# The opening of a two-layer diffusion backbone: modulation vectors on TensorE, six feed-forward tiles fed before the norm is known

## The chip, the cores and the metric

The kernel runs on one NeuronCore of one Trainium2 chip. Its time is the device time of one execution in microseconds (us). All operands are 32-bit floats. The engines are called as the profile calls them: PE (TensorE, matrix products) with PEld (its weight loads), DVE (VectorE), ACT (ScalarE), POOL (GpSimd), and SP, whose queue issues the DMA transfers.

## What is computed

Two layers work on 384 tokens (128 of a context, 256 of a latent grid) of width 1024. Each layer is a half-step feed-forward block, a token mixer, and another half-step feed-forward block. Ahead of each block stands an RMS norm whose result is scaled and shifted by vectors that come from a condition vector:

```python
def modulation(cvec, w, b):
    m = jax.nn.silu(cvec) @ w + b
    return m.reshape(cvec.shape[0], N_SUB, 3, D_MODEL)

def sub_in(x, g, m, sidx):
    shift, scale = m[:, sidx, 0], m[:, sidx, 1]
    return rmsnorm(x, g[sidx]) * (1 + scale[:, None, :]) + shift[:, None, :]

def swiglu(h, w_gu, w_down):
    gt, up = jnp.split(h @ w_gu, 2, axis=-1)
    return (jax.nn.silu(gt) * up) @ w_down
```

Context tokens and latent tokens have a condition vector each, so every scale and shift exists twice. The first block needs the shift and the scale of sub-layer 0 (1024 values each, twice) before its input is complete. This case is about that opening.

## The kernel before

**Layout.** The activations stand transposed: `X` has 128 partitions (a slice of the width) by 8 blocks `k` by 384 tokens. A tile of weights is 128 x 1024, 512 KB; its eight 128 x 128 pieces belong to the eight blocks `k`.

**Products in three parts.** Every factor is split into a rounded part `hi` and a remainder `lo`. `weights` loads a tile (DMA), rounds it on ACT (`hi`) and subtracts on DVE (`lo`). The input is split in the same way into `hh` and `hl`. A product of one tile with one block, called a pair below, is then three matrix products: hi·hh, hi·hl, lo·hh, each with 384 token columns.

**Order.** Engines run their instructions in order. A scheduler sets that order from a simulated timeline and from dependences that the code adds by hand: `chain("pe", ...)` strings matrix products in the order in which the code issues them, `chain("fill", ...)` does so for DVE. In the opening the order is written in the string `SPROG`, a list of tokens, each a step on a block.

**The opening (`start`).** Before the change:

- `A`: DVE computes the scale of block 0; then `stats` sums the squares of all blocks on PE (`L294`) and DVE takes the reciprocal root. `N` (`norm_end`) spreads that over the partitions by three products (`L267`), and ACT copies it to `R`. The squares themselves are taken before, on ACT, and added on DVE (`L282`).
- `S k`: the shift of block `k`, six of the eight on PE. Eight products with the condition vector as weights (two columns) and the loaded tile `mc` (`mod_w`) as data give a row of 2 x 128; ACT copies the row (`L1063`). `T k` turns that row into a column by a small product with the identity; ACT adds the bias (`L1071`).
- `H k` (`gen`): the scale of block `k` on DVE: two products with sums over 1024 elements (`mod_dot`, `L203`), one for each condition vector, then `L1085`. The `lo` parts of the first six gate/up tiles (`L164`, tile `gr`) are strung in here. Then `hgen` makes the normalised, scaled and shifted input of block `k` and splits it.
- `P k` (`step`): pairs of the tiles whose turn `GUP` gives, with block `k`; a tile that joins late catches up. The six tiles hold six PSUM banks to the end.

After the opening `ffn` evacuates the six banks (`evac`) and runs the remaining gate/up tiles, two at a time (`plain`, `L176` to `L178`), on the complete `hh` and `hl`.

Other blocks of the same kernel begin differently (`head`): their first tiles work on the input before the norm (`X` times scale only), with two more columns that hold the shift (`AUG`, 386 columns). The banks are multiplied by `R` when they are evacuated (`ev`), and the complete input is made by `hgen` afterwards for the tiles that follow.

Of the kernel before, what the change touches and what calls it, by code (L numbers as in the profile page):

```python
# [86 lines left out]
class Net:  # L87
# [98 lines left out]

    def mod_pe(self, l, n):
        nc = self.nc
        raw = self.wp.tile([P, 1024], F32, tag="raw", name="raw", bufs=3)
        nc.sync.dma_start(raw, self.a["mod_w"][l, n])  # L190
        ps = self.misc()
        for k in range(KD):
            nc.tensor.matmul(ps[:, :2], lhsT=raw[:, k * P:(k + 1) * P], rhs=self.sT[:, k, :], start=k == 0, stop=k == KD - 1)
        st, k = divmod(n, KD)
        nc.vector.tensor_copy(self.mod[l, st // 3, st % 3][:, k, :], ps[:, :2])
# [74 lines left out]

    def square(self, m):
# [8 lines left out]
        nc.scalar.activation(q, self.X[:, m, :], AF.Square)  # L280
        if not first:
            nc.vector.tensor_tensor(out=self.acc, in0=self.acc, in1=q, op=ALU.add)  # L282

# [3 lines left out]

    def stats(self):
        nc = self.nc
        ps = self.misc()  # L290
        st = ps[:, N:]
        for i in range(3):
            c = slice(i * P, (i + 1) * P)
            self.chain("pe", nc.tensor.matmul(st[:, i:i + 1], lhsT=self.acc[:, c], rhs=self.ones[:, 0:1], start=True, stop=True))  # L294
# [716 lines left out]
    def start(self, B=6):  # L1011
        nc, a = self.nc, self.a
        mm = lambda *args, **kw: self.chain("pe", nc.tensor.matmul(*args, **kw))  # L1013
# [4 lines left out]
        if PB:
            cr = self.fp.tile([P, 1024], F32, tag="junk", name="junk", bufs=1)[0:2, :]
            sel = T_([2, 2, P], F32, name="sel")  # L1020
            nc.sync.dma_start(cr, a["cv"])
            nc.sync.dma_start(sel, a["sel"])
        nc.sync.dma_start(self.small, a["small"])
# [4 lines left out]
        nc.scalar.activation(self.sT.rearrange("p k v -> p (k v)"), self.sm("cvec"), AF.Silu)  # L1028
        if PB:
            nc.scalar.activation(cr, cr, AF.Silu)  # L1030
            for v in range(2):
                for c in (slice(0, 512), slice(512, 1024)):
                    b = self.bank()
                    nc.tensor.matmul(b, lhsT=sel[:, v, :], rhs=cr[:, c], start=True, stop=True)
                    nc.scalar.activation(self.sb[:, v, c], b, AF.Copy)
        else:
            self.load_cond()
        for k in range(KD):
            self.square(k)
# [4 lines left out]
        tiles = []
        for k in range(KD):
            for o, dst in ((KD, sc), (0, sh)):
                dst[k] = T_([P, D], F32, tag="mc", name="mc", bufs=12)
                nc.sync.dma_start(dst[k], a["mod_w"][0, o + k])
            for _ in range(GUP.count(k)):
                tiles.append(self.gu_tile(0, 0, len(tiles), T_([P, D], F32, tag="gr", name="gr", bufs=B)))  # L1050
# [4 lines left out]
        def shift(k, src=None):
            if src is None:
                if k >= SHP:
                    return
# [4 lines left out]
            nc.scalar.activation(row[k], tr[0:2, :P], AF.Copy)  # L1063

        def turn(k):
            if k >= SHP:
                self.mod_dot(0, k, sh[k])
                nc.vector.tensor_scalar(out=S[:, k, :], in0=S[:, k, :], scalar1=self.sm("mod_b", k, 1), scalar2=None, op0=ALU.add)
                return
            mm(tn[:, 2 * k:2 * k + 2], lhsT=row[k], rhs=self.ident[0:2, 0:2], start=True, stop=True)  # L1070
            nc.scalar.activation(S[:, k, :], tn[:, 2 * k:2 * k + 2], AF.Identity, bias=self.sm("mod_b", k, 1))  # L1071

        def scale(k):
            if k in CP:
                return
            self.mod_dot(0, KD + k, sc[k])
            scale_end(k, G[:, k, :])

        def scale_pe(k):
            mm(tn[:, 64 + 2 * k:64 + 2 * k + 2], lhsT=row[k], rhs=self.ident[0:2, 0:2], start=True, stop=True)  # L1080
            scale_end(k, tn[:, 64 + 2 * k:64 + 2 * k + 2])

        def scale_end(k, src):
# [1 line left out]
            nc.vector.scalar_tensor_tensor(out=G[:, k, :], in0=src, scalar=one[:, k:k + 1], in1=g, op0=ALU.add, op1=ALU.mult)  # L1085
# [23 lines left out]
        def first():  # L1109
            self.last["fill"] = None  # L1110
            scale(0)
            self.stats()

        def second():
            self.norm_end()
            self.last["fill"] = self.dg

        tn = None
        for tok in SPROG.split():
            k = int(tok[1:] or 0)  # L1120
            if tok[0] in "TD" and tn is None:
                tn = self.misc()
            {"S": lambda: shift(k), "C": lambda: shift(k, sc[k]), "D": lambda: scale_pe(k), "T": lambda: turn(k), "H": lambda: gen(k), "P": lambda: step(k),
             "A": first, "N": second}[tok[0]]()
        return banks
# [128 lines left out]
```

## Time and profile before

| | us |
|---|---|
| three runs, median | 1421.05 |
| three runs, lowest and highest | 1419.83, 1423.15 |
| profiled execution, its own time | 1424.8 |
| span of the profiled execution | 1423.0 |

| engine | busy us | share of the span |
|---|---|---|
| PE | 1390.6 | 98% |
| PEld | 1349.1 | 95% |
| DVE | 1076.7 | 76% |
| ACT | 657.0 | 46% |

PE is busy nearly all the time; weight loads run beside the products. The profiled execution took 3.75 us more than the median of the three runs. Times inside the profile count from the start of its span. A line such as L203 is a line of the kernel before; in the changed kernel the same function stands some lines higher or lower.

### The profile page before, as it was taken

To read this page: it belongs to the slowest core of one execution; us is meant where nothing else is said; L and a number is where in the kernel's file an instruction comes from. 1 tells how busy PE (TensorE), PEld (TensorE's weight loads), DVE (VectorE), ACT (ScalarE), POOL (GpSimd) and SP (SyncE) were. 2 spreads that over 40 slices of the span, in tenths; PEclk is the share of its full clock that TensorE was granted. 3 is DMA by queue.
4 is the path that set the end of the run, shared out by engine and by line. 5 is a ranking of instruction groups with operands and counts; after the bars stand their busy time and mean duration, and the time that the engine had idled before them with its cause. 6 is when DMAs were issued, how large, how long until landed. Compare 5 with 4: busy or idle time off the path is not lost.

```text
span 1423.0 us, 20761 instructions
## 1 busy us (share of the span) xinstructions
PE 1390.6 (98%) x7877; PEld 1349.1 (95%) x7877; DVE 1076.7 (76%) x1945; ACT 657.0 (46%) x1079; POOL 10.8 (1%) x25
## 2 busy tenths in 40 slices
PE   7999999999998999999999999999998999999997
PEld 4999999998887999999999999999998999999886
DVE  7799989977987798879858887897688675334324
ACT  5443433339985643333345333333677564333322
POOL 0000000000110000000000000000000000000000
PEclk9999999999999999999999999999999999999999
DMA  9377777762135387767725766675330335333431
GB/s 372 131 258 246 230 225 249 237 204 89 60 119 178 105 256 231 216 200 246 241 74 189 246 210 210 211 243 186 104 114 31 103 121 162 125 127 120 133 104 45
DMA packets 71484, 247.24 MB, mean 174 GB/s; under 512 B 7877, under 2 KB 10583, under 8 KB 71385
## 3 DMA queue, kind: packets, MB, share of 16 engines
q1 hardware_dynamic: 71384, 245.92, 53.4%
q8 instruction: 62, 1.02, 0.3%
q14 instruction: 38, 0.30, 0.1%
HBM read 244.03 MB, written 1.85 MB: 173 GB/s over the span
## 4 chain that ended last, share of the span: by engine, by line
PE 91%; ACT 3%; DVE 3%; DMA 1%; issue 1%; SPq 0%; DVEq 0%; ACTq 0%
PE b L178 25%; PE b L176 25%; PE b L177 25%; PE b L737 5%; PE b L492 5%; PE b L1013 2%; PE m L737 1%; ACT rrt L495 1%; ACT ttt L495 1%; DMA sb<-in_cv 1%; DVE lo L164 0%; DVE lo L499 0%; ACT L495 0%; DMA raw<-in_lru_w_out 0%; DMA X<-in_x 0%
## 5 line engine op out<-in xcount | busy, mean ns | idle before, releaser
L163 ACT ACTIVATE hi<-raw 128x1024 fp32r<-128x1024 f32 (+1 forms) x282 | 293.3, 1042 | 599.7 <-issue 307.8
L178 PE MATMUL b<-hh,lo 128*128 128x384 f32 (+1 forms) x1372 | 461.9, 337 | 0.0
L176 PE MATMUL b<-hh,hi 128*128 128x384 f32 (+1 forms) x1372 | 461.0, 338 | 0.0
L177 PE MATMUL b<-hh,hi 128*128 128x384 f32 (+1 forms) x1372 | 456.6, 333 | 0.0
L164 DVE TENSOR_TENSOR lo<-raw,hi 128x1024 fp32r<-128x1024 f32 (+1 forms) x282 | 338.0, 1200 | 147.9 <-ACT hi L163 144.7
L203 DVE CUSTOM_DVE_ANT_0 junk<-mraw,sb 128x1024 f32<-128x1024 f32 x256 | 312.5, 1221 | 6.3 <-DMA mraw<-in_mod_w 3.5
L177 PEld LDWEIGHTS b<-hh,hi 128*128 128x128 f32 x1372 | 258.2, 188 | 0.0
L178 PEld LDWEIGHTS b<-hh,lo 128*128 128x128 f32 x1372 | 257.5, 188 | 0.0
L176 PEld LDWEIGHTS b<-hh,hi 128*128 128x128 f32 x1372 | 257.4, 188 | 0.0
L176 PE MATMUL b<-hid,hi 128*128 128x384 f32 x528 | 176.4, 334 | 0.0
L177 PE MATMUL b<-hid,hi 128*128 128x384 f32 x528 | 176.4, 334 | 0.0
L178 PE MATMUL b<-hid,lo 128*128 128x384 f32 x528 | 176.4, 334 | 0.0
L176 PEld LDWEIGHTS b<-hid,hi 128*128 128x128 f32 x528 | 99.1, 188 | 0.0
L177 PEld LDWEIGHTS b<-hid,hi 128*128 128x128 f32 x528 | 99.1, 188 | 0.0
L178 PEld LDWEIGHTS b<-hid,lo 128*128 128x128 f32 x528 | 99.1, 188 | 0.0
L393 DVE TENSOR_TENSOR t<-t,b 128x384 f32<-128x384 f32 x79 | 43.5, 552 | 71.1 <-PE b L178 71.0
L492 PE MATMUL b<-hh,hi 128*128 128x386 f32 x328 | 89.4, 354 | 6.0 <-DVE X L499 5.8
L492 PEld LDWEIGHTS b<-hh,hi 128*128 128x128 f32 x328 | 61.5, 195 | 9.1 <-issue 5.6
L492 PE MATMUL b<-hh,lo 128*128 128x386 f32 x164 | 56.8, 346 | 0.0
L178 PE MATMUL b<-hi,hid 128*128 128x512 f32 x132 | 51.4, 389 | 0.0
L177 PE MATMUL b<-lo,hid 128*128 128x512 f32 x132 | 51.4, 389 | 0.0
L176 PE MATMUL b<-hi,hid 128*128 128x512 f32 x132 | 51.3, 389 | 0.0
(218 smaller groups left out, 1534.9 us busy)
## 6 DMA issues: line engine op xcount, KB each, us to landing
raw<-in_gu SPq DMA_DIRECT2D x170, 512.0 KB, 4.1
mraw<-in_mod_w SPq DMA_DIRECT2D x128, 512.0 KB, 4.3
raw<-in_down SPq DMA_DIRECT2D x48, 512.0 KB, 4.3
raw<-in_down_last SPq DMA_DIRECT2D x22, 512.0 KB, 3.6
raw<-in_down SPq DMA_DIRECT2D x24, 384.0 KB, 4.2
mc<-in_mod_w SPq DMA_DIRECT2D x16, 512.0 KB, 10.2
raw<-in_lru_w_in SPq DMA_DIRECT2D x16, 512.0 KB, 3.7
raw<-in_w_qkv SPq DMA_DIRECT2D x10, 512.0 KB, 3.9
```

What stands on the lines that cost most here:

```text
L163: nc.scalar.activation(hi[:, :cols], raw[:, :cols], AF.Copy)
L164: self.wlo = nc.vector.tensor_tensor(out=lo[:, :cols], in0=raw[:, :cols], in1=hi[:, :cols].bitcast(F32), op=ALU.subtract)
L176: first = mm(out, lhsT=lh, rhs=rh, start=start, stop=False)
L177: mm(out, lhsT=lh, rhs=rl, start=False, stop=False)
L178: self.end = mm(out, lhsT=ll, rhs=rh, start=False, stop=stop)
L203: i = nc.vector.tensor_tensor_reduce(out=junk, in0=raw, in1=self.sb[:, v, :], scale=1.0, scalar=0.0, op0=ALU.mult, op1=ALU.add, accum_out= ...
L393: nc.vector.tensor_tensor(out=x, in0=x, in1=bu[:, ALL], op=ALU.mult)
L492: return self.chain("pe", nc.tensor.matmul(*args, **kw))
L495: return self.chain("act", nc.scalar.activation(*args, **kw))
L737: return self.chain("pe", T.matmul(*args, **kw)) if PIN else T.matmul(*args, **kw)
L1013: mm = lambda *args, **kw: self.chain("pe", nc.tensor.matmul(*args, **kw))
```

## The change

The opening is rewritten, and nothing else:

- **Scale on PE.** All eight scale vectors (`c0` to `c7`) and three of the shift vectors (blocks 4, 6, 7, `SPE`) come from PE. The condition vector is widened to 32 columns (`sT`, 30 of them zero), and the eight products of a vector write to four strips of 32 PSUM partitions in turn, two to a strip (`rows`); such eight products are called a row set below. ACT copies the 128 x 128 result, and `turn`, one product with a 0/1 matrix `sel4`, adds the four strips and gives a column. It stands directly behind its row set on PE.
- **Shift on DVE.** The other five shift vectors (blocks 0, 1, 2, 3, 5) are computed on DVE by `mod_dot`, where the eight scale vectors and the shifts of blocks 6 and 7 were.
- **Input before the norm.** The six tiles no longer take the normalised input. `gen` makes `X` times scale; `bias` casts the shift to two more columns; `pair` uses 386 columns. The squares (`Q`), `stats` (`X`) and `norm_end` (`N`) move to the end of the opening. `L` does the last two blocks of all six tiles.
- **After the opening** `ffn` runs `hgen` for blocks 0 to 5, `ev` for the six banks (which multiplies by `R`), then `hgen` for blocks 6 and 7.
- **Loads** are issued in the order of `LOADS`: the small vectors first, then `X` in four parts between the weights.

The order of PE where the last blocks stand. Before, a row set (`mc`, `sT`) and a turned row (`ident`, `row`) stand between pairs, and the turned row is that of an earlier row set:

```order
L1013 MATMUL b_166<-mc_189,sT_81 2x128 x8
L1013 MATMUL m_289<-ident_78,row_287 128x2
L1013 MATMUL b_160<-hh_77,hi_173 128x384 x2
L1013 MATMUL b_160<-hh_77,lo_174 128x384
L1013 MATMUL b_166<-mc_199,sT_81 2x128 x8
L1013 MATMUL m_289<-ident_78,row_306 128x2
```

Now, ahead of the pairs of block 5, the sums of the squares and the row sets of shift 6 and scale 7, each with its own turn behind it:

```order
L283 MATMUL m_146<-ones_79,acc_258 128x1 x3
L1006 MATMUL b_145<-mc_215,sT_113 32x128 x8
L1006 MATMUL m_146<-sel4_112,row_518 128x2
L1006 MATMUL b_145<-mc_213,sT_113 32x128 x8
L1006 MATMUL m_146<-sel4_112,row_530 128x2
L1006 MATMUL b_139<-hh_77,hi_152 128x386 x2
L1006 MATMUL b_139<-hh_77,lo_153 128x386
```

What moved: the turn no longer follows other pairs, and the norm's sums, which stood ahead of everything, stand in the last third.

The end of the opening on PE, now: the spreading of the norm, the last row set, the first pair of `L`, and in it the first products of the first `plain` tile (`b_722`, weights `hi_718` and `lo_719`), which read the complete input of block 0:

```order
L254 MATMUL m_146<-dg_555,ones_79 128x128
L254 MATMUL m_146<-dg_558,ones_79 128x128
L1006 MATMUL b_145<-mc_217,sT_113 32x128 x8
L1006 MATMUL m_146<-sel4_112,row_577 128x2
L1006 MATMUL b_139<-hh_77,hi_152 128x386 x2
L1006 MATMUL b_139<-hh_77,lo_153 128x386
L173 MATMUL b_722<-hh_77,hi_718 128x384
L1006 MATMUL b_139<-hh_77,hi_152 128x386
L174 MATMUL b_722<-hh_77,hi_718 128x384
L175 MATMUL b_722<-hh_77,lo_719 128x384
```

What moved: before, the first `plain` product stood behind 108 products of the six tiles, on an input that had been complete since `H 0`; now 33 products of the six tiles stand behind it.

DVE at its beginning. Before: the sums of squares, then the dots of scale 0 (two `ISA` rows are one dot):

```order
L282 TENSOR_TENSOR acc<-acc,t 128x384 x6
L203 ISA junk,m_83<-mc,sb 128x1024
L203 ISA m_83 128x1
L282 TENSOR_TENSOR acc<-acc,t 128x384
```

Now: the scale from PE's result (`L1060`), the remainder of X times scale (`L1071`), the dots of a shift (`L190`), its cast, then the weights' remainder:

```order
L1060 SCALAR_TENSOR_TENSOR m_83<-m,one,small 128x2
L1071 SCALAR_TENSOR_TENSOR hh<-X,m_83,hh 128x128
L1071 SCALAR_TENSOR_TENSOR hh<-X,m_83,hh 128x256
L190 ISA junk,m_82<-mc,sb 128x1024
L190 ISA m_82 128x1
L190 ISA junk,m_82<-mc,sb 128x1024
L190 ISA m_82 128x1
L1077 TENSOR_SCALAR m_82<-m_82,small 128x2
L166 CAST hh<-m_82 128x2
L169 TENSOR_TENSOR hh<-m_82,hh 128x2
L161 TENSOR_TENSOR lo<-gr,hi 128x1024 x2
```

What moved: DVE's first work now waits for PE, and every block's dots stand between the scale of that block and the scale of the next.

DVE where the norm arrives: the last scaled remainders (`L1071`), then `X` times `R` for six blocks (`L317`, `L309`), the cast (`L166`) and the remainder (`L169`) of the complete input of block 0:

```order
L1071 SCALAR_TENSOR_TENSOR hh<-X,m_83,hh 128x256
L317 TENSOR_TENSOR t<-X,R 128x384 x2
L309 SCALAR_TENSOR_TENSOR t<-X,m_83,R 128x128
L309 SCALAR_TENSOR_TENSOR t<-X,m_83,R 128x256
L317 TENSOR_TENSOR t<-X,R 128x384 x3
L166 CAST hh<-t 128x384
L166 CAST hh<-m_82 128x2
L166 CAST hh<-t 128x384
L314 SCALAR_TENSOR_TENSOR hh<-t,m_82,hh 128x128
L314 SCALAR_TENSOR_TENSOR hh<-t,m_82,hh 128x256
L169 TENSOR_TENSOR hh<-t,hh 128x384
```

What moved: these stood in the blocks `H 0` to `H 5`; now they follow each other at the end, behind `N`.

On ACT the order of the first steps changed too: before, the table load has no wait and is followed by the condition vector's activation; now the table load stands behind the wait for the transfer of `small`.

The diff, cut to what matters here:

```diff
-XO = [slice(0, 4), slice(4, 8)]
-SHP = 6
-GUP = (0, 1, 2, 3, 4, 5)
-SPROG = "A S0 N S1 T0 H0 S2 T1 H1 P0 S3 T2 H2 P1 S4 T3 H3 P2 S5 T4 H4 P3 T5 H5 P4 P5 T6 H6 T7 H7 P6 P7"
+SPE = (4, 6, 7)
+GUP = (0, 0, 1, 2, 3, 3)
+LOADS = "x0 c0 g0 c1 s0 g1 x2 c2 s1 g2 x4 c3 s2 g3 x6 c4 s3 g4 c5 s4 g5 c6 s5 c7 s6 s7"
+SPROG = "C0 T0 H0 C1 T1 H1 B0 Q0 Q1 C2 T2 P0 H2 B1 Q2 Q3 C3 T3 P1 H3 B2 C4 T4 P2 H4 B3 Q4 Q5 S4 U4 C5 T5 P3 H5 B4 Q6 Q7 C6 T6 P4 X H6 B5 S6 U6 C7 T7 P5 N B6 H7 S7 U7 B7 L"
...
         elif banks:
-            for j in range(hp):
-                evac(j, *banks[2 * j:2 * j + 2])
+            for k in range(KD - 2):
+                self.hgen(l, s, k)
+            for i in range(2 * hp):
+                ev(i, banks)
+            for k in range(KD - 2, KD):
+                self.hgen(l, s, k)
...
+        sel4 = T_([P, 2], F32, name="sel4")
+        sT = T_([P, KD, 32], F32, name="sT")
+        nc.gpsimd.memset(sT, 0.0)
         nc.sync.dma_start(self.small, a["small"])
-        for c in XO:
-            nc.sync.dma_start(self.X[:, c, :], a["x"][:, c, :])
+        nc.sync.dma_start(cr, a["cv"])
+        nc.sync.dma_start(sel, a["sel"])
+        nc.sync.dma_start(sel4, a["sel4"])
...
-        nc.scalar.activation(self.sT.rearrange("p k v -> p (k v)"), self.sm("cvec"), AF.Silu)
+        nc.scalar.activation(sT[:, :, 0:2], self.sm("cvec").rearrange("p (k v) -> p k v", v=2), AF.Silu)
...
+        def rows(t):
+            r = slice(len(row) % 4 * P, len(row) % 4 * P + P)
             for j in range(KD):
-                mm(tr[0:2, :P], lhsT=self.sT[:, j, :], rhs=src[:, j * P:(j + 1) * P], start=j == 0, stop=j == KD - 1)
-            row[k] = T_([2, P], F32, tag="row", name="row", bufs=3)
-            nc.scalar.activation(row[k], tr[0:2, :P], AF.Copy)
+                q = slice((j % 4) * 32, (j % 4) * 32 + 32)
+                mm(tr[q, r], lhsT=sT[:, j, :], rhs=got[t][:, j * P:(j + 1) * P], start=j < 4, stop=j >= 4, skip_group_check=True)
+            row[t] = T_([P, P], F32, tag="row", name="row", bufs=2)
+            nc.scalar.activation(row[t], tr[:, r], AF.Copy)
+
+        def turn(t):
+            o = 400 + 2 * int(t[1]) + (32 if t[0] == "s" else 0)
+            mm(tn[:, o:o + 2], lhsT=row[t], rhs=sel4, start=True, stop=True, skip_group_check=True)
+            return tn[:, o:o + 2]
...
+            fill(nc.vector.scalar_tensor_tensor(out=G[:, k, :], in0=turn(f"c{k}"), scalar=one[:, k:k + 1], in1=g,
+                                                op0=ALU.add, op1=ALU.mult))
+
+        def shift(k):
+            nc.scalar.activation(S[:, k, :], turn(f"s{k}"), AF.Identity, bias=self.sm("mod_b", k, 1))
+
+        def gen(k):
+            for g in range(2):
+                x, z = self.X[:, k, GRP[g]], G[:, k, g:g + 1]
+                hi = self.hh[:, k, GRP[g]]
+                nc.scalar.activation(hi, x, AF.Copy, scale=z)
+                fill(nc.vector.scalar_tensor_tensor(out=self.hl[:, k, GRP[g]], in0=x, scalar=z, in1=hi.bitcast(F32),
+                                                    op0=ALU.mult, op1=ALU.subtract))
+
+        def bias(k):
+            if k not in SPE:
+                self.mod_dot(0, k, got[f"s{k}"])
+                fill(nc.vector.tensor_scalar(out=S[:, k, :], in0=S[:, k, :], scalar1=self.sm("mod_b", k, 1), scalar2=None, op0=ALU.add))
+            fill(self.split(self.hh[:, k, N:NB], self.hl[:, k, N:NB], S[:, k, :], True))
+            for i in range(B):
+                if GUP[i] == k:
+                    fill(los[i])
 
         def pair(k, i):
...
-                mm(banks[i][:, ALL], lhsT=lh[:, c], rhs=rh[:, k, ALL], start=k == 0 and n == 0, stop=k == KD - 1 and n == 2)
+                mm(banks[i][:, AUG], lhsT=lh[:, c], rhs=rh[:, k, AUG], start=k == 0 and n == 0, stop=k == KD - 1 and n == 2)
...
-        def gen(k):
-            if k:
-                scale(k)
+        def last():
             for i in range(B):
-                if GUP[i] == k:
-                    self.chain("fill", los[i])
-            keep = self.last["fill"]
-            self.hgen(0, 0, k)
-            self.last["fill"] = keep
+                for k in (KD - 2, KD - 1):
+                    pair(k, i)
```

More of the change, by code (lines that the diff above doesn't have):

```diff
@@ L37 @@
 MF = (32, 16)
-MP = 0
 PROG = """
@@ L185, in mmk @@
         return self.mm3(out, w[0][:, c], w[1][:, c], xh[:, k, cols], xl[:, k, cols], start, stop)
[L187 to L195, printed above, removed]
     def mod_dot(self, l, n, raw):
@@ L281, in square @@
         if not first:
-            nc.vector.tensor_tensor(out=self.acc, in0=self.acc, in1=q, op=ALU.add)
+            add = nc.vector.tensor_tensor(out=self.acc, in0=self.acc, in1=q, op=ALU.add)
+            if key:
+                self.chain(key, add)
     def norm(self):
@@ L1014, in start @@
         T_ = self.ph.tile
-        sh, sc = {}, {}
-        row = {}
+        got, row, tiles, los = {}, {}, [], []
         one = T_([P, KD], F32, name="one")
[L1018 to L1022, printed above, removed]
+        cr = self.fp.tile([P, 1024], F32, tag="junk", name="junk", bufs=1)[0:2, :]
+        sel = T_([2, 2, P], F32, name="sel")
@@ L1029, in start @@
[L1029 to L1039, printed above, removed]
+        nc.scalar.activation(sT[:, :, 0:2], self.sm("cvec").rearrange("p (k v) -> p k v", v=2), AF.Silu)
@@ L1040, in start @@
+        nc.scalar.activation(cr, cr, AF.Silu)
+        for v in range(2):
+            for c in (slice(0, 512), slice(512, 1024)):
+                b = self.bank()
+                nc.tensor.matmul(b, lhsT=sel[:, v, :], rhs=cr[:, c], start=True, stop=True)
+                nc.scalar.activation(self.sb[:, v, c], b, AF.Copy)
         nc.vector.tensor_scalar(out=one, in0=self.sm("mod_b", KD, KD), scalar1=1.0, scalar2=None, op0=ALU.add)
-        los = []
         banks = [self.bank() for _ in range(B)]
-        tr = self.bank()
@@ L1044, in start @@
[L1044 to L1050, printed above, removed]
+        tr, tn = self.bank(), self.misc()
+        for tok in LOADS.split():
+            c, k = tok[0], int(tok[1])
+            if c == "x":
+                nc.sync.dma_start(self.X[:, k:k + 2, :], a["x"][:, k:k + 2, :])
+            elif c == "g":
+                tiles.append(self.gu_tile(0, 0, k, T_([P, D], F32, tag="gr", name="gr", bufs=B)))
@@ L1065, in turn @@
[L1065 to L1071, printed above, removed]
-        def scale(k):
[L1074 to L1083, printed above, removed]
-            g = self.sm("norm_g", k, 1).to_broadcast([P, 2])
-            nc.vector.scalar_tensor_tensor(out=G[:, k, :], in0=src, scalar=one[:, k:k + 1], in1=g, op0=ALU.add, op1=ALU.mult)
+        fill = lambda i: self.chain("fill", i)
+        def rows(t):
+            r = slice(len(row) % 4 * P, len(row) % 4 * P + P)
+            for j in range(KD):
+                q = slice((j % 4) * 32, (j % 4) * 32 + 32)
+                mm(tr[q, r], lhsT=sT[:, j, :], rhs=got[t][:, j * P:(j + 1) * P], start=j < 4, stop=j >= 4, skip_group_check=True)
+            row[t] = T_([P, P], F32, tag="row", name="row", bufs=2)
+            nc.scalar.activation(row[t], tr[:, r], AF.Copy)
@@ L1097, in step @@
                         pair(j, i)
-        def gen(k):
-            if k:
-                scale(k)
+        def last():
             for i in range(B):
-                if GUP[i] == k:
-                    self.chain("fill", los[i])
-            keep = self.last["fill"]
-            self.hgen(0, 0, k)
-            self.last["fill"] = keep
[L1109 to L1118, printed above, removed]
-        for tok in SPROG.split():
[L1120 to L1124, printed above, removed]
+                for k in (KD - 2, KD - 1):
+                    pair(k, i)
+        ops = {"C": lambda k: rows(f"c{k}"), "S": lambda k: rows(f"s{k}"), "T": scale, "U": shift, "H": gen, "B": bias, "P": step,
+               "Q": lambda k: self.square(k, "fill")}
+        rest = {"X": lambda: self.stats(tn), "N": self.norm_end, "L": last}
+        for tok in SPROG.split():
+            if tok in rest:
+                rest[tok]()
+            else:
+                ops[tok[0]](int(tok[1:]))
         return banks
@@ L1131, in run @@
         self.nst = self.res.tile([P, 16], F32, name="nst")
-        self.fillq = [(0, n) for n in range(16, 72) if MP == 0 or n // KD != 7] + [(1, n) for n in range(72)]
+        self.fillq = [(0, n) for n in range(16, 72)] + [(1, n) for n in range(72)]
         with self.filling():
@@ L1184 @@
     h["cv"] = np.ascontiguousarray(cv)
+    sel4 = np.zeros((P, 2), np.float32)
+    sel4[np.arange(4) * 32, 0] = sel4[np.arange(4) * 32 + 1, 1] = 1.0
+    h["sel4"] = sel4
     parts = {
@@ L1194 @@
     mod = np.ascontiguousarray(mw.transpose(0, 2, 1).reshape(2, NTM, P, D))
-    mod[0, :SHP] = wtiles(mw[0, :, :SHP * P])
-    for k in CP:
-        mod[0, KD + k] = wtiles(mw[0, :, (KD + k) * P:(KD + k + 1) * P])[0]
-    if MP:
-        mod[0, 7 * KD:8 * KD] = wtiles(mw[0, :, 7 * D:8 * D])
+    for n in SPE + tuple(range(KD, 2 * KD)):
+        mod[0, n] = wtiles(mw[0, :, n * P:(n + 1) * P])[0]
     h["mod_w"] = mod
```

18 lines of the change are left out of this document (7 added, 11 removed).

## The prediction

> **What bounds the kernel now.** I read the page first (busy time, the chain that ended last).
>
> ```profile
> PE 1390.6 (98%) x7877; PEld 1349.1 (95%) x7877; DVE 1076.7 (76%) x1945; ACT 657.0 (46%) x1079; POOL 10.8 (1%) x25
> PE 91%; ACT 3%; DVE 3%; DMA 1%; issue 1%; SPq 0%; DVEq 0%; ACTq 0%
> ```
>
> PE bounds it: what PE loses in the opening has nowhere to come back. Next, PE's waits, in the first 70 us (four rows) and after them (the largest row).
>
> ```profile
> PE b L1034 <- ACT junk L1030: 3.4, 1, 3.4
> PE m L294 <- DVE acc L282: 2.7, 1, 2.7
> PE b L1013 <- DVE hh L172: 2.6, 1, 2.6
> PE b L1013 <- DVE hh L169: 1.3, 1, 1.3
> PE b L492 <- DVE X L499: 5.8, 3, 3.1
> ```
>
> After 70 us no wait is over 5.8 us in all, and it is for DVE work that itself hangs on PE. So a delay of the opening goes through to the end. I measure the opening by an *offset*: the time at which PE does a product, minus the products done by then times their pitch. The PE timeline gives it.
>
> ```profile
> 24.79 0.45 PE L1013 MATMUL b<-hh,hi 128*128 128x384 f32 x1 [1.29 <-DVE hh L169]
> 55.65 0.34 PE L176 MATMUL b<-hh,hi 128*128 128x384 f32 x1
> 56.17 0.34 PE L176 MATMUL b<-hh,hi 128*128 128x384 f32 x1
> ```
>
> Three products from 55.65 to 56.17: 0.1735 each. Before 55.65 stand 108 products of the six tiles: offset 55.65 - 108 x 0.1735 = 36.9. The windows tell what filled those 37 us (columns: PE, PEld, DVE, ACT, POOL, granted clock, DMA share, GB/s).
>
> ```profile
> 20.00:25.00 5.00, 3.66 (x30) 2.55 (x27) 5.00 (x10) 3.93 (x10) 0.00 (x0) 1.00 1.03 410
> 25.00:30.00 5.00, 2.43 (x11) 1.27 (x11) 5.00 (x11) 1.82 (x2) 0.00 (x0) 0.83 1.02 406
> 35.00:40.00 5.00, 5.00 (x36) 4.17 (x34) 5.00 (x12) 2.88 (x6) 0.00 (x0) 1.00 1.03 409
> ```
>
> DVE is full from 20 to 40, PE is not: in the opening DVE is the bound, until PE has its inputs.
>
> **The change, step by step.** *Start.* Rows of ACT, of SP's queue, of the DMA issues and of PE:
>
> ```profile
> 0.73 1.28 ACT L1030 ACT_TABLE_LOAD   x1 [0.73 <-PEq L1236]
> 2.34 1.05 ACT L1030 ACTIVATE junk<-junk 2x1024 f32<-2x1024 f32 x1 [0.33 <-DMA junk<-in_cv]
> 3.60 0.21 ACT L1028 ACTIVATE sT<-small 128x16 f32<-128x16 f32 x1 [0.20 <-DMA small<-in_small]
> 0.73 0.36 SPq L1021 DMA_DIRECT2D junk<-in_cv  x1
> 1.44 0.36 SPq L1023 DMA_DIRECT2D small<-in_small  x1
> small<-in_small SPq DMA_DIRECT2D x1, 161.0 KB, 2.1
> 3.45 7.19 PE L1034 MATMUL b<-junk,sel 2*128 2x512 f32 x8 [3.45 <-ACT junk L1030]
> ```
>
> `small` is now issued first, at 0.73, and lands 2.1 later, at 2.85. The table load waits for it: 2.85 + 1.28 + 0.21 (`sT`) + 1.05 = 5.4, against 3.39. The broadcast products start 2.0 later and end at 5.4 + 7.2 = 12.6. `C0` stands behind them. The added `sel4` load and POOL's zeroing of `sT` lie beside the wait for `small`: nothing; without that cover a fraction of a microsecond.
>
> *A row set.* Eight products in four column strips have no row. Nearest rows: a set in one place, in its short and its long form; its weight loads; the turn; the copy of a row on ACT.
>
> ```profile
> 21.28 1.91 PE L1013 MATMUL b<-mc,sT 128*2 128x128 f32 x16
> 14.66 3.55 PE L1013 MATMUL b<-mc,sT 128*2 128x128 f32 x16
> L1013 PEld LDWEIGHTS b<-mc,sT 128*2 128x2 f32 x96 | 8.8, 97 | 4.8 <-issue 0.5 <-ACT hh L171 0.2
> 23.11 0.38 PE L1013 MATMUL m<-ident,row 2*128 2x2 f32 x2
> L1063 ACT ACTIVATE row<-b 2x128 f32<-2x128 f32 x6 | 1.6, 264 | 8.9 <-PE b L1013 8.9
> ```
>
> Upper end 1.91, if strips don't run beside each other. Lower end 1.91/4 = 0.48, if four do. The loads took 8.8 us for six sets, two of them in the long form, 1.86 times 1.91: 8.8/(4 + 2 x 1.86) = 1.14 a set, if loads never overlap. I take 0.8, midway between 0.48 and 1.14. The turn directly behind adds, all on PE's path: row copy 0.26, turn 0.38, some 0.35 of hops between engines: 1.8 a set.
> The Trainium skill, "TensorE: Matmul & The Clock Gate", section "Measured speedup vs the span model", has three column strips of 32 running 2.38 times as fast as one after the other; 1.91/2.38 = 0.80 would be its estimate, and the sum would stay as it is. No row here shows strips at all, so the trace neither bears it out nor speaks against it.
>
> *First scale.* The long form stood behind a wait of PE at 14.66 (the window from 25 to 30, where PE waited most, shows a granted clock of 0.83), and `C0` stands where it did, so I take 0.8 x 1.86 = 1.5: 12.6 + 1.5 + 0.26 + 0.38 + 0.26 hops = 15.0. Until then DVE's strung work cannot begin. Before, its first dot stood at 11.5:
>
> ```profile
> 11.48 1.22 DVE L203 CUSTOM_DVE_ANT_0 junk<-mc,sb 128x1024 f32<-128x1024 f32 x1
> ```
>
> Bounds: in the short form 0.7 less.
>
> *DVE's blocks.* Its rows, and those of the ACT step that it waits for:
>
> ```profile
> L203 DVE CUSTOM_DVE_ANT_0 junk<-mc,sb 128x1024 f32<-128x1024 f32 x20 | 24.4, 1218 | 0.1
> L1085 DVE SCALAR_TENSOR_TENSOR m<-m,one,small 128x2 f32<-128x2 f32 x8 | 1.7, 217 | 0.1
> L307 ACT ACTIVATE hh<-X,m 128x128 fp32r<-128x128 f32 x32 | 12.4, 387 | 2.0 <-DVE X L342 2.0
> L308 DVE SCALAR_TENSOR_TENSOR hh<-X,m,hh 128x256 fp32r<-128x256 f32 x32 | 15.4, 480 | 0.0
> L308 DVE SCALAR_TENSOR_TENSOR hh<-X,m,hh 128x128 fp32r<-128x128 f32 x32 | 11.1, 347 | 0.7 <-ACT hh L307 0.7
> L164 DVE TENSOR_TENSOR lo<-gr,hi 128x1024 fp32r<-128x1024 f32 x6 | 7.3, 1219 | 0.0
> L282 DVE TENSOR_TENSOR acc<-acc,t 128x384 f32<-128x384 f32 x35 | 19.4, 553 | 4.4 <-ACT t L280 3.8
> ```
>
> `H`: scale 0.22, wait for ACT 0.5 (0.39 and a hop), remainders 0.35 + 0.48: 1.55. `B`: two dots 2.44, and bias, cast and difference on two columns, 0.2 each (nearest row 0.22): 3.05. Together 4.6. Ten of twenty dots are gone, 12.2 us of DVE. But `H` and `B` stand in one strung row, so DVE idles while ACT casts.
> `H0` ends at 16.6. `T1` follows at 17.4 (ACT first does two casts and two squares for block 0, then `C1`'s row copy), `H1` ends at 19.3 with ACT's queue, `B0` at 22.4. `P0` starts there, 2.4 earlier than before (24.79). Then two remainders of weights and an addition, 2.8 (each overlaps the next by 0.08): 25.2; + 4.6 = 29.8 (`P1`); one remainder and two additions 2.2, + 4.6 = 36.6 (`P2`); one more and a block, 5.7: 42.3 (input of `P3`). On PE: `P2` has 18 products, 3.1, then `S4 U4 C5 T5`, 3.6: 43.3 or, with the input, 43.4.
>
> *From 43.4 PE is the bound again.* What it has left and what comes in between; rows of the sums, of the spreading, of `R`, and of the steps of the complete input:
>
> ```profile
> 13.33 1.41 PE L294 MATMUL m<-ones,acc 128*128 128x1 f32 x6 [2.69 <-DVE acc L282]
> 18.15 0.94 PE L267 MATMUL m<-dg,ones 128*128 128x128 f32 x6
> L300 ACT ACTIVATE R<-m 128x384 f32<-128x384 f32 x5 | 2.5, 491 | 29.8 <-PE m L267 29.8
> 29.41 0.74 DVE L320 SCALAR_TENSOR_TENSOR t<-X,m,R 128x128 f32<-128x128 f32 x2
> 30.07 1.49 DVE L328 TENSOR_TENSOR t<-X,R 128x384 f32<-128x384 f32 x3
> L169 DVE CAST hh<-t 128x384 fp32r<-128x384 f32 x10 | 3.3, 354 | 0.0
> L172 DVE TENSOR_TENSOR hh<-t,hh 128x384 fp32r<-128x384 f32 x30 | 16.1, 553 | 11.1 <-ACT hh L171 11.1
> ```
>
> `P3` 36 products, 6.25; `P4` and `P5` 18 each, 6.25; four sets with turns (`C6 S6 C7 S7`) 7.2; the sums 1.41/1.86 = 0.76; the spreading 0.94; the first pair of `L` 0.52: 43.4 + 21.9 = 65.3. The next product is `L173`, a `plain` one in the midst of `L`, and it needs the complete input of block 0. That hangs on `N`, whose spreading ended 0.52 + 1.8 earlier, at 63.0: `R` 0.49, then DVE makes `X` times `R` for all six blocks, 5 x 0.50 + 0.74 = 3.2, then the cast 0.35, hops 0.2: 67.2, so PE waits 1.9. `L174` needs the remainder: 0.74 + 0.55 and a little, 1.4. Queued behind both are the other 33 products of `L`, which wait for nothing. Bounds of this wait: 0, if DVE's order lets block 0 through sooner, to 3.3.
>
> *Sum.* 111 products are done by then: 65.3 - 111 x 0.1735 + 3.3 = 49.3. The 386th column costs 144 x 0.1735 x 2/384 = 0.13. Offset 49.5 against 36.9: **+12.6**. On the profiled execution, 1424.8, that makes 1437.4; that execution is 3.75 over the median, so against the runs 1421.05 + 12.6 = **1433.6**.
> Bounds: a set at 0.48 takes 0.32 off each of four, of `S4` and `C5` (as far as DVE doesn't hide them) and 0.6 off `C0`: -2.5. The wait gone: -3.3. `C0` in the short form: -0.7. All together +6, still slower. A set at 1.91: four by 1.1, 4.4; the two before `P3`, 2.2; `C0`, 2.1: +8.7.
>
> **Rivals.**
> *Strips run one after another*: 1433.6 + 8.7 = 1442. For it: no row here shows a product that gains by writing to a part of the partitions only. Against: the four strips are distinct columns of the array. Chance 0.14.
> *The wait in `L` vanishes and sets are cheap*: 1427 to 1430. For it: the scheduler's order can only make DVE's row begin earlier. Against: seven steps stand ahead of the cast in DVE's order. 0.12.
> *Faster: the 12.2 us that DVE is spared come through in full.* One mechanism: ACT and PE run ahead of DVE, so that `P3` starts when its tiles are there and not at 43.4. At 410 GB/s a tile of 512 KB takes 1.28, `X` 3.8; 17 tiles and `X` from 2.9 on, with the first transfer's 2.1, put `P3` at 30.6 at the earliest: 1433.6 - 12.8 = 1420.8, and 1417.5 if the wait in `L` goes too. It decides at a `P3` before 31. For it: DVE was 100% busy in the windows above. Against: the order holds each scale behind the dots of the block ahead of it, so DVE is fed only from 15.0 on. 0.11.
> *The same: the delay is made up later.* It would need waits of 12 us after the opening that shrink; the largest is 5.8, and behind PE's own work. 0.05.
>
> **How the numbers follow.** My forecast, `P3` near 43 with some of the wait, has 0.58 and its own range 1430 to 1437. About 0.2%, 2.8 us, is what a measurement of this kernel can tell from no change. The faster rival gives 0.08 to faster and 0.03 to same, the last one 0.05 to same; the rest, 0.84, is slower. The range 1426 to 1443 takes in the first two rivals and leaves out the last two.
>
> **What would show it.** Right: the first broadcast at 5.4 us; DVE idle until about 15; `P0` near 22 and `P3` near 43; row sets of 0.6 to 1.0 us, each followed by 0.6 to 1 us without PE products, waiting for ACT's row; near 65 a wait of `L173` for DVE of about 2 us, and of `L174`; after it a stream without waits, its offset near 49. Wrong: sets of 1.9; `P3` before 31, with DVE idle between blocks rather than PE; or the offset back near 37 at 100 us.

## The result and the profile after

| kernel | median us | runs | ratio to before, 95% interval |
|---|---|---|---|
| before, beside the changed kernel | 1422.10 | 4 | |
| changed | 1437.68 | 4 | 1.0104 [1.0087, 1.0122] |
| changed, once more (`after_again`) | 1435.93 | 6 | 1.0094 [1.0076, 1.0113] |

The change makes the kernel about 15 us slower. The profiled execution took 1441.11 (span 1438.4); that of before 1424.8.

Busy time and the chain of the changed kernel, from its page:

```profile
PE 1396.9 (97%) x7967; PEld 1354.9 (94%) x7967; DVE 1076.2 (75%) x1975; ACT 665.0 (46%) x1100; POOL 11.1 (1%) x26
PE 90%; ACT 4%; DVE 4%; DMA 1%; issue 1%; ACTq 0%; SPq 0%; DVEq 0%
```

PE is busy 6.3 us longer than before (1396.9 against 1390.6), and it waits longer. PE's waits in the first 85 us:

```profile
PE m L1006 <- ACT row L1051: 6.2, 11, 1.1
PE b L1026 <- ACT junk L1022: 5.6, 1, 5.6
PE b L1006 <- DVE hh L166: 4.8, 3, 2.5
PE b L173 <- DVE hh L166: 1.7, 1, 1.7
PE b L174 <- DVE hh L169: 0.7, 1, 0.7
PE b L1006 <- DVE lo L161: 0.3, 1, 0.3
```

19.3 us in all, against 10.0 before; 9.3 us more of waiting and 6.3 of busy time make up the 15.4 us by which the span grew. None of these waits is for a transfer. The largest row is new: eleven turns, each waiting for ACT's copy of the row set just ahead of it. The added busy time is no added work of the feed-forward tiles, whose products are the same in number: part of them took longer (see the first experiment).

The offset (as in the prediction: the start of PE's n-th product of 384 or 386 columns, less n-1 pitches of 0.1735) is worked out from PE's timeline:

| product | before | changed | changed, once more |
|---|---|---|---|
| 36 | 36.4 | 35.6 | 34.6 |
| 72 | 36.9 | 38.9 | 37.6 |
| 108 | 36.9 | 45.6 | 42.7 |
| 148 | 36.9 | 53.8 | 49.8 |
| 400 | 36.9 | 53.8 | 49.7 |
| 1400 | 36.7 | 53.6 | 49.6 |

All is lost between product 36 and product 148, between about 42 and 80 us. From there to product 5500 (1021 us) the distance to before stays at 16.9 to 17.0 in the first profile and at 12.8 to 13.0 in the second. In the second token mixer 1.6 and 3.2 us of it come back, and it ends at 15.4 and 9.6.

### The profile page after: what moved, and what is told of

The parts are those of the page before. It is cut to its first block, busy times and chain, and to the rows that moved or that the text cites. A ratio compares the mean times of both kernels' runs of the same rounds, so it can differ in the third digit from the quotient of the medians.

```text
span 1438.4 us, 21015 instructions
## 1 busy us (share of the span) xinstructions
PE 1396.9 (97%) x7967; PEld 1354.9 (94%) x7967; DVE 1076.2 (75%) x1975; ACT 665.0 (46%) x1100; POOL 11.1 (1%) x26
## 4 chain that ended last, share of the span: by engine, by line
PE 90%; ACT 4%; DVE 4%; DMA 1%; issue 1%; ACTq 0%; SPq 0%; DVEq 0%
PE b L175 25%; PE b L173 25%; PE b L174 25%; PE b L485 5%; PE b L730 5%; PE b L1006 2%; PE m L730 1%; ACT rrt L488 1%; ACT ttt L488 1%; PE b L1026 0%; DVE junk L190 0%; DMA sb<-in_cv 0%; DVE lo L161 0%; DVE lo L492 0%; ACT L488 0%
## 5 line engine op out<-in xcount | busy, mean ns | idle before, releaser
L173 PE MATMUL b<-hh,hi 128*128 128x384 f32 (+1 forms) x1372 | 460.9, 338 | 1.7 <-DVE hh L166 1.7
L174 PE MATMUL b<-hh,hi 128*128 128x384 f32 (+1 forms) x1372 | 457.0, 333 | 0.7 <-DVE hh L169 0.7
L190 DVE CUSTOM_DVE_ANT_0 junk<-mraw,sb 128x1024 f32<-128x1024 f32 x256 | 312.9, 1222 | 11.1 <-DMA mraw<-in_mod_w 8.2
L173 PEld LDWEIGHTS b<-hh,hi 128*128 128x128 f32 x1372 | 257.4, 188 | 2.0 <-issue 2.0
L174 PEld LDWEIGHTS b<-hh,hi 128*128 128x128 f32 x1372 | 258.3, 188 | 1.1 <-DVE hh L169 1.1
L173 PE MATMUL b<-hid,hi 128*128 128x384 f32 x528 | 176.4, 334 | 0.0
L174 PE MATMUL b<-hid,hi 128*128 128x384 f32 x528 | 176.4, 334 | 0.0
L173 PEld LDWEIGHTS b<-hid,hi 128*128 128x128 f32 x528 | 99.1, 188 | 0.0
L174 PEld LDWEIGHTS b<-hid,hi 128*128 128x128 f32 x528 | 99.1, 188 | 0.0
L382 DVE TENSOR_TENSOR t<-t,b 128x384 f32<-128x384 f32 x76 | 41.9, 552 | 67.3 <-PE b L175 67.2
L168 ACT ACTIVATE hid<-t 128x384 fp32r<-128x384 f32 x88 | 45.5, 517 | 20.1 <-DVE t L382 19.2
L175 PE MATMUL b<-hi,hid 128*128 128x512 f32 x132 | 51.4, 389 | 0.0
L174 PE MATMUL b<-lo,hid 128*128 128x512 f32 x132 | 51.4, 389 | 0.0
```

What stands on the lines that cost most here:

```text
L168: self.nc.scalar.activation(hi, src, AF.Copy)
L173: first = mm(out, lhsT=lh, rhs=rh, start=start, stop=False)
L174: mm(out, lhsT=lh, rhs=rl, start=False, stop=False)
L175: self.end = mm(out, lhsT=ll, rhs=rh, start=False, stop=stop)
L190: i = nc.vector.tensor_tensor_reduce(out=junk, in0=raw, in1=self.sb[:, v, :], scale=1.0, scalar=0.0, op0=ALU.mult, op1=ALU.add, accum_out= ...
L382: nc.vector.tensor_tensor(out=x, in0=x, in1=bu[:, ALL], op=ALU.mult)
```

## The experiments

Each kernel is the changed one with the edit shown, unless it says otherwise. "Offset" is that at 200 products. Two profiles of the unchanged new opening give 53.8 and 49.8, so a single offset is read only to about 4 us, and the waits beside it. By time alone, of the kernels made from the changed one only four can be told from it, whose two intervals reach from 1.0076 to 1.0122: one strip, without dots, and the two with all vectors from PE. The changes of order are read from their waits.

**The changed kernel again.**

> The changed kernel once more, beside the next ones on the same chip, to see how much of its opening repeats. Theory: the waits and steps up to 80 us repeat to 0.1 us; only where PE has products at 0.325 instead of 0.1735 apart may differ, so the offset is 48 to 54. Rival: the opening itself varies by several us between executions, and no difference of single profiles below that may be read.

PE's rows at the fourth step and at the first `plain` products, of this profile and then of the changed kernel's first one:

```profile
43.71 0.60 PE L1006 MATMUL b<-hh,hi 128*128 128x386 f32 x2
66.37 0.41 PE L173 MATMUL b<-hh,hi 128*128 128x384 f32 x1 [1.71 <-DVE hh L166]
67.74 0.69 PE L174 MATMUL b<-hh,hi 128*128 128x384 f32 x1 [0.78 <-DVE hh L169]
```

```profile
44.97 0.59 PE L1006 MATMUL b<-hh,hi 128*128 128x386 f32 x2
69.23 0.41 PE L173 MATMUL b<-hh,hi 128*128 128x384 f32 x1 [1.73 <-DVE hh L166]
70.61 0.69 PE L174 MATMUL b<-hh,hi 128*128 128x384 f32 x1 [0.70 <-DVE hh L169]
72.38 0.85 PE L1006 MATMUL b<-hh,hi 128*128 128x386 f32 x2
```

The waits repeat to 0.1 us but for one (ahead of `P2` 0.47 and 1.14, where `P2` starts at the same time in both), the offset does not: 53.8 against 49.8. The difference lies in long products. In a row like the last one two products take 0.64 to the next row, 0.32 each, where 0.1735 is the usual pitch. Of the products from 18 to 82 us, 52 are long in the first profile, 30 in the second, and none before the change. The 52 cost 52 x 0.147 = 7.6 us. The granted clock shows some of them (windows of the first profile; PEclk is the third column from the end):

```profile
35.00:40.00 5.00, 4.50 (x14) 4.42 (x15) 4.37 (x11) 2.67 (x4) 0.00 (x0) 1.00 1.02 407
60.00:65.00 5.00, 5.00 (x24) 4.97 (x23) 1.57 (x8) 0.81 (x2) 0.00 (x0) 0.72 0.00 0
70.00:75.00 5.00, 4.39 (x14) 4.39 (x15) 3.98 (x10) 5.00 (x11) 0.00 (x0) 0.50 0.01 3
```

PEclk is 0.72 and 0.50 in the two late windows, but 1.00 from 35 to 40, where the products were long too. The long products stand behind PE's waits. The Trainium skill, "TensorE: Matmul & The Clock Gate", section "What's actually happening", says that PE's clock is halved after idle time (a window of about 3.4 us) and that the window that decides it runs free of the kernel, so that the number of slow products differs from run to run. The two profiles agree in the second point: nearly the same waits, 52 and 30 long products. In the first they don't: no wait behind the first one is over 2.5 us, and products are long all the same. That the waits bring them about is argued, not shown: the nine long products at the start of `P5` in the first profile stand behind two waits of 0.46, and in the second profile none is long behind the same two.

**The start.**

```diff
-        nc.sync.dma_start(self.small, a["small"])
         nc.sync.dma_start(cr, a["cv"])
         nc.sync.dma_start(sel, a["sel"])
+        nc.sync.dma_start(self.small, a["small"])
...
+        nc.scalar.activation(cr, cr, AF.Silu)
         nc.scalar.activation(sT[:, :, 0:2], ...)
-        nc.scalar.activation(cr, cr, AF.Silu)
```

> The small vectors are loaded in the order of before (condition vector, selector, small), and ACT makes the condition vector's activation first, so that its table load waits for no transfer. Theory (every delay of the opening runs through to the end): the broadcast products start at 3.4 instead of 5.6, DVE's first scale at 12.7 instead of 14.8, the input of the fourth step 2.1 earlier, and the offset at the end of the opening falls from 53.8 to about 51.7: 2 us less in all. Rival (the start is hidden behind the loads, which fill DMA to 43 us): the offset stays at 53 to 54.

1433.69 (ratio 1.0073 [1.0053, 1.0092]), offset 52.4. ACT's table load and PE's first products:

```profile
0.73 1.28 ACT L1021 ACT_TABLE_LOAD   x1 [0.73 <-PEq L1219]
3.43 7.19 PE L1026 MATMUL b<-junk,sel 2*128 2x512 f32 x8 [3.43 <-ACT junk L1021]
15.69 0.59 PE L1006 MATMUL m<-sel,row 128*128 128x2 f32 x2 [2.06 <-ACT row L1051]
```

The start is 2.1 earlier, as expected, but the second turn now waits 2.06 instead of 1.13 for ACT, and the first pairs come 1.2 earlier (20.8 against 22.0). Against the first profile, which has as many long products (52; here 51), the offset falls by 1.4: the theory, less what the next wait takes.

**The norm earlier.**

```diff
-... Q6 Q7 C6 T6 P4 X H6 B5 S6 U6 C7 T7 P5 N B6 ...
+... Q6 Q7 X C6 T6 P4 H6 B5 S6 U6 N C7 T7 P5 B6 ...
```

> Only the order tokens X and N stand earlier: the sums of the squares ahead of the set of scale 6, the spreading behind the turn of shift 6. The complete input of block 0 is then ready before the last products of the six tiles. Theory: PE's waits of the first plain products (1.7 and 0.7) vanish, and with them the long products behind them (16 at 0.325 instead of 0.1735, 2.4 us): offset 53.8 falls by 2.4 to 4.8. Rival 1 (the long products come from the opening's waits as a whole): only 2.4. Rival 2 (DVE's seven steps of the complete input now delay the scale of block 7, and PE waits there instead): no gain, offset 53 to 54.

1435.15 (1.0087 [1.0068, 1.0106]), offset 48.3. The waits of `L173` and `L174` are gone, but the last turn has a new one; PE's row, and ACT's rows ahead of its copy:

```profile
66.59 0.38 PE L1006 MATMUL m<-sel,row 128*128 128x2 f32 x2 [2.38 <-ACT row L1051]
```

```profile
62.55 2.73 ACT L319 ACTIVATE t<-t,m,m 128x128 f32<-128x128 f32 x6
65.18 0.79 ACT L1070 ACTIVATE hh<-X,m 128x128 fp32r<-128x128 f32 x2
65.87 0.51 ACT L168 ACTIVATE hh<-t 128x384 fp32r<-128x384 f32 x1
66.28 0.26 ACT L1051 ACTIVATE row<-b 128x128 f32<-128x128 f32 x1
```

ACT's steps of the complete input stand ahead of the row copy. That is the second rival with ACT in DVE's place: 1.7 + 0.7 went, 1.6 came back. No long products followed here (21 in all instead of 30 or 52); that is the gain of this profile. The times hardly show it: 1435.15 against 1437.68 and 1435.93.

**Turns apart from their row sets.**

```diff
-... S4 U4 C5 T5 P3 H5 B4 Q6 Q7 C6 T6 P4 X H6 B5 S6 U6 C7 T7 P5 N B6 H7 S7 U7 B7 L
+... S4 C5 U4 T5 C6 P3 H5 B4 Q6 Q7 T6 S6 P4 X H6 B5 U6 C7 S7 P5 T7 U7 N B6 H7 B7 L
```

> From the fourth step on each turn stands behind another row set or behind a step's pairs, not directly behind its own row set; nothing else moves. Theory: the waits of the turns for ACT's copy there (six of 0.46, one of 0.75) go but for one or two, and the row sets stay at 0.65: offset 53.8 falls by 2 to 3, PE's waits for ACT's row from 6.2 to about 3.5 in all. Rival (the copy is not what holds PE; the row set's end is modelled too early and the wait moves into the sets): the sets lengthen to 1.1 and the offset stays.

1433.30 (1.0071 [1.0053, 1.0088]), offset 47.2. PE's waits in the first 90 us, in part:

```profile
PE m L1006 <- ACT row L1051: 3.2, 5, 1.1
PE b L174 <- DVE hh L169: 1.9, 1, 1.9
PE b L1006 <- ACT row L1051: 0.9, 2, 0.5
```

The turns' waits fall by 3.0, as the theory says; two come back as row sets that wait (0.9: a set directly behind another waits until ACT has copied the first; both write to the same tile `b`, to different columns), and `L174` waits 1.9 instead of 0.7. All waits of PE together fall only from 19.3 to 18.7.

**One strip.**

```diff
-                q = slice((j % 4) * 32, (j % 4) * 32 + 32)
-                mm(tr[q, r], ..., start=j < 4, stop=j >= 4, ...)
+                mm(tr[0:32, r], ..., start=j == 0, stop=j == KD - 1, ...)
```

> All eight products of a row set write to one strip of 32 partitions instead of four strips in turn; ACT copies 32 partitions. Theory (four strips run beside each other): a set takes 1.9 instead of 0.65 (3.5 instead of 1.08 in the long form), and the offset rises by 1.25 for each of the four late sets, 2.5 for the two ahead of the fourth step, and about 2 at the start: 53.8 to 61 to 64, some 8 to 10 us more. Rival (the 32 columns of weights in place of two are what makes the set shorter, not the strips): the sets stay near 0.65 and the time stays.

1444.00 (1.0148 [1.0125, 1.0171]), offset 57.2. A late set of this kernel, and the same set of the changed kernel:

```profile
53.64 1.93 PE L1006 MATMUL b<-mc,sT 128*32 128x128 f32 x16
```

```profile
51.53 0.65 PE L1006 MATMUL b<-mc,sT 128*32 128x128 f32 x16
```

Four strips run beside each other: 1.93/0.65, 3.0 times as fast. The 32 columns in place of two cost nothing by themselves (1.91 before). The offset rises by 3.4 to 7.4 and the time by 6 to 8, less than the 8 to 10 of the theory: beside the longer sets only 7 products are long instead of 30 or 52, and PE's waits are 16.8 instead of 19.3.

**The three orders together**: the start as above, turns apart, and the spreading ahead of the pairs of block 5.

```diff
+... S4 C5 U4 T5 C6 P3 H5 B4 Q6 Q7 T6 S6 P4 U6 X H6 B6 C7 S7 B5 T7 U7 H7 B7 N P5 L
```

> The three changes of order together: small vectors loaded third, turns apart from their row sets from the fourth step on, and the norm's spreading ahead of the pairs of block 5, so that the complete input is ready before the first plain product. Theory: the gains add as far as they are separate terms: offset near 43 (53.8 less 2 for the start, 3 for the turns, 3 to 5 for the plain products), still above 37, since DVE's blocks hold the first four steps: time about 6 us above the kernel before. Rival (the terms cover each other; removing one uncovers the next wait): offset 46 to 48.

1432.83 (1.0072 [1.0058, 1.0086]), offset 47.0: the rival. The terms cover each other. New waits, from PE's list:

```profile
PE m L1006 <- ACT row L1051: 4.3, 5, 2.3
PE m L254 <- DVE dg L248: 1.7, 1, 1.7
```

**Without DVE's dots.**

```diff
+        nc.gpsimd.memset(self.mod[0, 0, 0], 0.0)
...
-                self.mod_dot(0, k, got[f"s{k}"])
```

> The changed kernel without the ten sums over 1024 that DVE makes for the shifts of blocks 0, 1, 2, 3 and 5 (those shifts are then the bias alone); everything else and its order as in the changed kernel. Theory (DVE's blocks of 4.6 hold the first four steps): blocks of 2.1, first pairs at 19.5 instead of 22, the fourth step's input at 32 instead of 42; PE then reaches P3 at 36 to 38 instead of 45, and the offset falls by 6 to 9 to 45 to 48. Rival (DVE's dots are hidden; PE's turns and products in the long form set the pace): P3 stays at 43 to 45 and the offset within 2 us.

1428.51 (1.0045 [1.0028, 1.0063]), offset 43.6. First pairs and fourth step:

```profile
19.59 1.01 PE L1006 MATMUL b<-hh,hi 128*128 128x386 f32 x2
36.28 0.60 PE L1006 MATMUL b<-hh,hi 128*128 128x386 f32 x2
```

In the steps PE waits for DVE only once, 0.3 for a weights' remainder, and the fourth starts 7.4 to 8.7 earlier. So DVE's dots between the scales held the first half, as the theory says; 6 to 10 us of the offset. Even without them it is 6.7 us over that of before, with these among the waits that are left:

```profile
PE b L1027 <- ACT junk L1023: 5.7, 1, 5.7
PE m L1006 <- ACT row L1052: 5.6, 11, 1.1
PE b L173 <- DVE hh L166: 2.0, 1, 2.0
```

**All vectors from PE.** No dots in the opening, no broadcast products ahead of the first set; the loads follow the new order, and there are four row buffers instead of two.

```diff
-SPE = (4, 6, 7)
-GUP = (0, 0, 1, 2, 3, 3)
+SPE = tuple(range(8))
+GUP = (0, 1, 2, 3, 4, 5)
+SPROG = "C0 S0 T0 U0 H0 B0 Q0 C1 S1 P0 T1 U1 H1 B1 Q1 ... C6 S6 C7 S7 P5 X T6 U6 H6 B6 T7 U7 H7 B7 N L"
```

> All eight shifts come from PE too, so that DVE makes no sum over 1024 in the opening; the condition vector's broadcast to 128 partitions, needed later only, is a DMA transfer behind the weights instead of products ahead of the first row set; one tile joins with each block, and each block's two row sets stand ahead of the pairs of the block before. Theory (PE's late start and DVE's blocks in one strung row are what holds the opening, and row sets are cheap): first pairs near 12 instead of 22, P5 near 37, offset 27 to 34, under the 37 of before: 1412 to 1419. Rival 1 (PE is the bound with 16 sets and turns in the long form): offset 38 to 44, 1423 to 1430. Rival 2 (the transfers are): PE waits for tiles mc up to 40 us, offset 33 to 40.

1430.29 (1.0047 [1.0031, 1.0064]), offset 42.7. Its waits, in part:

```profile
PE b L1006 <- DMA mc<-in_mod_w: 7.4, 1, 7.4
PE b L1006 <- ACT row L1043: 4.9, 9, 1.1
PE m L1006 <- DVE m L1052: 2.4, 6, 0.5
```

The first rival's number, but not its reason: PE is not full. Nine sets wait for ACT's copy of the set ahead, six turns for DVE.

**The same, with the pairs of a step in parts and a row set on both sides.**

```diff
+SPROG = "C0 S0 T0 H0 Q0 U0 B0 C1 p00 S1 T1 H1 Q1 U1 B1 C2 p10 S2 T2 H2 Q2 p11 U2 B2 C3 p201 S3 T3 ... C7 U6 B6 p54 N S7 T7 H7 p55 U7 B7 L"
```

(`p201` is the pairs of block 2 with tiles 0 and 1.)

> All sixteen vectors from PE as in the run of that name, but in another order: a block's first row set stands ahead of one half of the pairs of the block before and its second set behind it, so that ACT's copies and the turns lie beside pairs; the first block's set is loaded before X; the sums of the squares and the spreading stand ahead of the last tile's pairs; the activation of the broadcast condition vector stands behind the complete input. Theory (what is left there are PE's waits for ACT between sets and turns, some 9 us, and long products after them): offset 42.6 falls to 31 to 36, under the 37 of before: 1415 to 1421. Rival (sixteen sets and turns fill PE, and the transfers set the pace up to 40 us, whatever the order): 38 to 42, 1424 to 1429.

1420.44, 12 runs (0.9988 [0.9975, 1.0000]), offset 35.0. Its waits:

```profile
PE b L1009 <- DMA mc<-in_mod_w: 7.9, 2, 5.9
PE m L1009 <- DVE m L1055: 0.8, 2, 0.4
PE b L1009 <- DVE hh L166: 0.5, 2, 0.3
```

Behind the first loads hardly a wait is left, and 5 products are long. Offset and time are the theory's. This is the fastest of the kernels, though no more than 0.25% faster than before, and by the interval perhaps not at all. It keeps the input before the norm and the row sets in strips, with more of them than the changed kernel, so neither is by itself what made that one slower. What it does without is DVE's dots, the broadcast ahead of the first set, and the order of the changed kernel.

**Strips alone, in the kernel before.**

```diff
-                mm(tr[0:2, :P], lhsT=self.sT[:, j, :], ...)
+                mm(tr[q, :P], lhsT=sT[:, j, :], ..., start=j < 4, stop=j >= 4, ...)
```

> The kernel before with one part of the change alone: its six row sets in four strips of 32 with the product that adds the strips, instead of two columns in one place. Theory (before, DVE sets the pace until 45 us and PE has time to spare there): PE has 7 us less work in the opening and waits more; offset 36 to 37.5, the time that of before within 0.2%. Rival (PE's work in the opening counts): offset 32 to 34, 3 to 5 us faster.

1423.49 (1.0004 [0.9989, 1.0018]), offset 36.4 against 36.9: the theory. DVE is still full, as the windows of this kernel show:

```profile
20.00:30.00 10.00, 7.49 (x51) 5.29 (x48) 10.00 (x22) 5.26 (x13) 0.00 (x0) 1.00 1.02 407
30.00:40.00 10.00, 8.71 (x50) 6.99 (x52) 9.96 (x19) 5.61 (x10) 0.00 (x0) 1.00 1.03 409
```

But not all of the saved work turned into waiting. PE's waits grew by 1.7 only, from 10.0 to 11.7, and 18 products are long here, about 2.6 us, where none was before.

**Strips and four scales from PE, in the kernel before.**

```diff
-CP = ()
+CP = (2, 3, 4, 5)
```

(with the strips of the last one, and in `SPROG` `T2 C2 P0 S3 D2 H2` and the like for these blocks.)

> The kernel before with row sets in four strips and the scales of blocks 2 to 5 from PE (ten dots fewer by eight of twenty on DVE), each set and its turn on both sides of a step's pairs; the norm stays at the beginning, the input normalised, the loads as before. Theory (the part of the change that helps is taking dots off DVE, where nothing new waits in one row with it): DVE's blocks shrink by 2.4 for four blocks, PE's products run together from 28 us on, offset 32 to 35: 2 to 5 us faster than before. Rival (the added turns make PE and DVE wait for each other as in the changed kernel): offset 37 or more.

1422.22 (1.0004 [0.9989, 1.0020]), offset 35.7. In its window from 30 to 40 DVE is busy 5.53 of 10 instead of 9.96. That window, the start of PE's first pairs, and PE's waits behind it:

```profile
30.00:40.00 10.00, 9.19 (x96) 7.73 (x96) 5.53 (x9) 6.09 (x13) 0.00 (x0) 1.00 1.03 409
24.74 1.25 PE L1013 MATMUL b<-hh,hi 128*128 128x384 f32 x2
PE m L1013 <- DVE m L1090: 1.2, 3, 0.4
```

Neither the theory's 2 to 5 us nor the rival's 37: the offset is 1.2 lower and the time that of before. The trace shows what is left once DVE has room. PE's first pairs start where they did (24.74 against 24.79), and from there to the first `plain` product PE waits only 1.2 us; the rest is PE's own row of products, which now holds four sets and turns more.

## Why the prediction was right, step by step

It foretold 1433.6 (1426 to 1443) and slower; measured were 1437.68 and 1435.93, 14 to 16 us slower where +12.6 was said. DVE's first scale, the last step of the fourth block's input, and PE's starts of the first row set and the steps, of the changed kernel:

```profile
5.56 7.19 PE L1026 MATMUL b<-junk,sel 2*128 2x512 f32 x8 [5.56 <-ACT junk L1022]
12.68 1.08 PE L1006 MATMUL b<-mc,sT 128*32 128x128 f32 x16
14.79 0.22 DVE L1060 SCALAR_TENSOR_TENSOR m<-m,one,small 128x2 f32<-128x2 f32 x1 [11.53 <-PE m L1006]
22.02 1.01 PE L1006 MATMUL b<-hh,hi 128*128 128x386 f32 x2 [2.49 <-DVE hh L166]
29.32 1.01 PE L1006 MATMUL b<-hh,hi 128*128 128x386 f32 x2 [1.82 <-DVE hh L166]
36.08 1.01 PE L1006 MATMUL b<-hh,hi 128*128 128x386 f32 x2 [0.47 <-DVE hh L166]
41.76 0.16 DVE L169 TENSOR_TENSOR hh<-m,hh 128x2 fp32r<-128x2 f32 x1
```

| step | foretold | measured |
|---|---|---|
| broadcast products start | 5.4 | 5.56 |
| first scale on DVE | 15.0 | 14.8 |
| P0, P1, P2 | 22.4, 29.8, 36.6 | 22.0, 29.3, 36.1 |
| input of P3 | 42.3 | 41.9 |
| P3 starts | 43.4 | 45.0 and 43.7 |
| first `plain` product | 67.2 | 69.2 and 66.4 |
| its wait, and that of the next | 1.9 and 1.4 | 1.7 and 0.7; 1.7 and 0.8 |
| offset | 49.5 | 53.8 and 49.8 |

- *The start, DVE's blocks, the serial sets and turns, the wait in `L`*: right in place, and each seen to go when a run takes it away: the start by 2.1 (`e1_table`), `P3` 7.4 to 8.7 earlier (`e7_nodots`), 3.0 of the turns' waits (`e3_apart`), both waits in `L` (`e2_norm`). The start and DVE's blocks were right in size to 0.5 us; the two waits in `L` together were 2.4 instead of 3.3.
- *The row set* was mis-sized: 0.8 assumed, 0.65 measured (1.08 instead of 1.5 in the long form). With their turns and waits the four late ones took 5.9 instead of 7.2.
- *The term that was missing*: the products were all taken at 0.1735. In the first profile `P2`'s 18 products took 5.8 instead of 3.1, so that `P3` started at 45.0; half of `P5`'s 18 and 17 behind the wait of `L173` were long as well. These are 1.6 + 9 x 0.15 + 17 x 0.15 = 5.5 us; in the second profile 30 products are long instead of 52. The prediction let `C0` alone be long, though it had the row that showed what follows a wait. It also set beside that row a window that isn't its own: the set at 14.66 lies in these two, where the granted clock shows 1.00, and from 10 to 15 PE was busy even less than from 25 to 30 (2.31 and 2.43).

```profile
10.00:15.00 5.00, 2.31 (x9) 1.57 (x9) 4.53 (x11) 2.63 (x5) 0.00 (x0) 1.00 1.03 417
15.00:20.00 5.00, 5.00 (x32) 3.17 (x30) 4.58 (x17) 1.81 (x3) 0.00 (x0) 1.00 1.02 408
```

- *Luck*: cheap sets (1.3) and short waits in `L` (0.9) stood against the long products. So the 4.3 us by which the first profile's offset missed are a net, and the second profile's 49.8 lies beside 49.5 because the two sides nearly cancelled there.
- *Strips one after another* (0.14): refuted, sets of 0.65; `e4_strip`, which makes them so, took 1444.00 where this rival said 1442. *No wait in `L`, cheap sets* (0.12): the sets were cheaper, the waits stayed. *The faster rival* (0.11): `P3` at 45.0 and 43.7, not before 31; DVE's order was the reason, as `e7_nodots` shows, and with its dots gone the kernel is still slower, with the waits at the start, of the turns and in `L`.
- *The delay made up later* (0.05): refuted by the offset, 53.8 at product 400 and 53.6 at 1400; the second token mixer gave back 1.6 and 3.2 us, and why was not looked into.
